# An encoder layer's MLP: the second transposing transfer a step pair later, and another block order in the down projection

## The chip, the cores and the metric

The kernel runs on one NeuronCore of a Trainium2 chip. The metric is the device time of one execution in microseconds (us). Before the change three executions took 1333.12, 1335.69 and 1338.51 us; their median, 1335.69 us, is the time that the change is held against.

## What is computed

One layer of a hybrid encoder: x has 256 tokens of 2048 features, float32. An attention mixer comes first (a combined input projection, two attention branches, gates, an output projection). Its code is not touched. The last part is the MLP, which the change concerns:

```python
h = rms_norm(x, norm_mlp_pre[l])
u = jnp.square(jax.nn.relu(jnp.einsum('bsd,df->bsf', h, w_up[l])))
x = x + rms_norm(jnp.einsum('bsf,fd->bsd', u, w_down[l]), norm_mlp_post[l])
```

w_up is 2048 x 8192 and w_down 8192 x 2048, both float32. We call the two products Up and Down.

## The kernel before the change

**Products in three parts.** Every float32 operand is split into a high part (rounded to the tensor engine's fp32r type, on ScalarE: ACT) and a low remainder (on VectorE: DVE). A product of two 128-row blocks is three matmuls: high by high, high by low, low by high (`Products.add`, L786, matmuls at L793). All of Up and Down runs in *steps*. A step has one weight tile of 128 x 4 x 512 elements (1 MB), that is a 2 x 2 pattern of blocks against a 2 x 2 pattern of activation blocks. A step is done either in eight block products (`eight`, 24 matmuls) or, after Strassen, in seven (`seven`, 21 matmuls) with sums of blocks on both sides. Each weight tile is loaded on SyncE's queue (SP, L700) and split on ACT and DVE (L710 and L712, or L715 to L729 for a step in seven), two steps before its use (`Weights.next`).

**Up** goes through eight groups of 1024 columns, each in eight steps, order `UPS`: weight tiles 1, 2, 0, 4, 3, 6, 5, 7, of which 0 and 3 are steps in seven. The text names steps by n = 0 to 7. A group has two *column groups* (cg) of 512 columns; there are NG = 16 of them. The result z of a group (after ReLU) is turned into operands for Down while the next group runs (`up_each`): `sent` copies the two 16-bit halves of z into planes on ACT (L736) and issues a transposing DMA on SP's queue (L738); `joined` puts the halves together again on ACT (L743); a Square follows (L1307); `u_sets` (via `act_sets`, L1168) makes the operand set. Both column groups are sent in step n = 1 and joined in n = 3 and n = 5. The last group's column groups (14 and 15) are turned by matmuls instead (`u_T`), inside Down.

**Operand sets.** An even cg is used in seven: its set is two pairs of tiles (high `ah`, low `al`), one of single blocks and one of sums of blocks (`sm`, on DVE). An odd cg has one pair. A set of an even cg in `FIRST` (12 and 14 before) has one more block, copied and subtracted at L1191 and L1192, because some of its steps are done in eight. Every set is stored to DRAM on GpSimd's queue (`keeph`, `keepl`, L1195), and read again on ACT's queue when it is needed (`act_again`, tiles `bh`, `bl`, L1208).

**Down** makes its 2048 output columns in two halves, g = 0 and 1. Each half sums over the 16 column groups in eight *blocks* of two, four steps a block (`down_steps`), three matmuls a product, in strict order on the tensor engine (`pr.in_order`). The lists `blocks` give the order:

```python
blocks = [[12, 0, 2, 4, 6, 8, 10, 14],      # first half
          [14, 0, 2, 4, 6, 8, 10, 12]]      # second half
```

Block 12 comes first in the first half, with sets that `u_sets` left in memory. While it runs, 14 and 15 are transposed; while the second block runs, `u_sets` makes and stores their sets (14 in its step n = 1, 15 in n = 3). At step n = 0 of every block but the last, `act_again` asks for the next block's sets. The second half begins with the block that ended the first, whose sets are still there.

**What orders the work.** All these tiles (sets, planes, transposed data, weight sums and lows) are *pages* of 4 KB a partition from one pool of 27. The tile framework orders each engine's instructions from the program's order and its own model of time; an instruction that finds no free page waits, and later ones may pass it. So the code's place of a step is where it may begin, not where it runs. On each engine and queue the resulting order is then fixed.

The functions, with the line numbers that the profile uses:

Of the kernel before, what the change touches and what calls it, by code (L numbers as in the profile page):

```python
# [51 lines left out]
def encoder_layer(ctx: ExitStack, tc: tile.TileContext, a, out):  # L52
# [13 lines left out]
    def page(shape, dt, name):  # L66
        return pages.tile(shape, dt, tag="pg", name=name)
# [673 lines left out]
    def joined(got, dst):  # L741

        nc.scalar.copy(  # L743
            dst.rearrange("p k q -> p (k q)")
            .bitcast(U16)
            .rearrange("p (k t q h) -> p t h k q", k=4, t=2, h=2),
            got.rearrange("p (t h k) q -> p t h k q", t=2, h=2),
        )
# [411 lines left out]


    NG = DFF // 512
    FIRST = (NG - 4, NG - 2)

    def seven_of(cg):
        return cg % 2 == 0

    def act_sets(cg, u):  # L1168


        srcs = []
        if seven_of(cg):
            a11, a21 = u[:, 0:2, :P], u[:, 0:2, P:]
            a12, a22 = u[:, 2:4, :P], u[:, 2:4, P:]
            sums = page([P, 4, 2, P], F32, f"sm{cg}")
            nc.vector.tensor_sub(sums[:, 0], a21, a22)
            nc.vector.tensor_sub(sums[:, 1], a11, a21)
            nc.vector.tensor_sub(sums[:, 2], sums[:, 0], a11)
            nc.vector.tensor_add(sums[:, 3], a12, sums[:, 2])
            own = [(slice(0, 1), a11.unsqueeze(1)),  # L1180
                   (slice(1, 3), u[:, 2:4].rearrange("p k (t q) -> p t k q", t=2))]
            if cg in FIRST:
                own.append((slice(3, 4), a21.unsqueeze(1)))
            srcs = [([P, 1 + len(own), 2, P], own), ([P, 4, 2, P], [(slice(0, 4), sums)])]
        else:
            srcs = [([P, 4, T], [(slice(0, 4), u)])]
        got = []
        for i, (shape, pieces) in enumerate(srcs):
            hi, lo = page(shape, F32R, f"ah{cg}{i}"), page(shape, F32R, f"al{cg}{i}")
            for at, src in pieces:  # L1190
                nc.scalar.copy(hi[:, at], src)  # L1191
                nc.vector.tensor_sub(lo[:, at], src, hi[:, at].bitcast(F32))  # L1192
            for n, part in (("h", hi), ("l", lo)):
                kd = dram.tile(shape, F32, name=f"keep{n}{cg}{i}", tag=f"keep{n}{cg}{i}")
                nc.gpsimd.dma_start(kd, part.bitcast(F32))  # L1195
                kept[cg, i, n] = (shape, kd)
            got.append([hi, lo])
        return got

    def act_again(cg, g):  # L1200

        out = []
        for i in range(2 if seven_of(cg) else 1):
            got = []
            for n in "hl":
                shape, kd = kept[cg, i, n]
                t = page(shape, F32R, f"b{n}{g}{cg}{i}")
                nc.scalar.dma_start(t.bitcast(F32), kd)  # L1208
                got.append(t)
            out.append(got)  # L1210
        return out

    sets = {}
# [27 lines left out]
    def u_sets(cg, u):  # L1241

        got = act_sets(cg, u)
        if NG - 4 <= cg < NG - 2:
            sets[0, cg] = got

    def u_piece(t, half, ps, summed, z):
# [18 lines left out]
            )  # L1266
    wd = a["w_down"].rearrange("(g h j p) c -> p h g j c", h=2, j=2, p=P)

    blocks = [[NG - 4] + list(range(0, NG - 4, 2)) + [NG - 2], [NG - 2] + list(range(0, NG - 2, 2))]

    def down_steps(g, bi):
        b = blocks[g][bi]
# [11 lines left out]
    for g in range(DFF // 1024):  # L1284
        z = Late(lambda g=g: [page([P, 2, 512], F32, f"u{g}{t}") for t in range(2)])

        def up_each(n, g=g, uz=uz):
            if not g:
                first_up(n)
                if n == 7:  # L1290
                    for i in (0, 3, 5):
                        f = page([P, 2, T], F32, f"h2f{i}")
                        for k in range(2):
                            d = hT2[i][:, k].bitcast(F32)
                            nc.vector.tensor_add(f[:, k], d[:, :T], d[:, T:])
                        h2sum[i] = sums_of(f[:, 0], f[:, 1], f"h2s{i}")
                return
            by_dma = g < DFF // 1024 - 1
            for c in range(2):
                cg = g * 2 - 2 + c  # L1300
                if by_dma and c in (0, 1):
                    if n == (1, 1)[c]:
                        uh[cg] = sent([uz[t][:, c] for t in range(2)], f"u{cg}")
                    if n == (3,5)[c]:
                        us[cg] = page([P, 4, T], F32, f"u{cg}")
                        joined(uh[cg], us[cg])
                        nc.scalar.activation(us[cg], us[cg], AF.Square)  # L1307
                elif n == c + 1:
                    us[cg] = u_T(cg, uz)
            steps = (3, 5) if by_dma else (1, 2)  # L1310
            if n in steps:
                cg = g * 2 - 2 + steps.index(n)
                u_sets(cg, us[cg])

        wide_group(
            f"u{g}",
            ups(g),
            uw,
            h2stat7,
            h2stat8,  # L1320
            (1, 2, 3, 7),
            z,
            partial(u_piece, z=z),
            each=up_each,
            turn=None if g else turn_rows,
            after={} if g else {2: scaled[0]},
        )
        uz = z
# [133 lines left out]
    for g in range(2):  # L1462
        pr = Products(f"p{g}", (1, 2, 3, 7))
        pr.in_order = True
        for bi, b in enumerate(blocks[g]):
            end = bi == len(blocks[g]) - 1
            for n, (cg, j, seven) in enumerate(down_steps(g, bi)):
                w = uw.next()
                if g == 0 and bi == 0 and n in (1, 2):
                    us[NG - 3 + n] = u_T(NG - 3 + n, uz)  # L1470
                if g == 0 and bi == 1 and n % 2:
                    u_sets(NG - 2 + n // 2, us[NG - 2 + n // 2])
                if n == 0:
                    for c in range(2):
                        if not end:
                            sets[g, blocks[g][bi + 1] + c] = act_again(blocks[g][bi + 1] + c, g)
                        elif not g:
                            sets[1, b + c] = sets[0, b + c]
                if g == 1 and bi == 5 and n == 0:
                    gp2 = [page([P, 1024], F32, f"gp2{h}") for h in range(2)]  # L1480
                    for h in range(2):
                        nc.sync.dma_start(
                            gp2[h],
                            a["g_mlp_post"][:, h * 1024 : (h + 1) * 1024].partition_broadcast(P),
                        )
                if end and g and n == 0:
                    x3 = [page([P, 1024], F32, f"x3{i}") for i in range(4)]
                    for i in range(4):
                        nc.scalar.dma_start(x3[i], kept["x", i])
                if g == 1 and bi == 6:  # L1490
                    gain(0, n // 2, n % 2)
                    if n % 2:
                        first_means(n // 2)
                if seven:
                    final = end and not any(s for _, _, s in down_steps(g, bi)[n + 1 :])
                    pr.seven(partial(dstat7, sets[g, cg], j), w, final)
                    if final:
                        for t in range(2):
                            zw[g, t] = page([P, 2, 512], F32, f"zw{g}{t}")
                        pr.combine([zw[g, t] for t in range(2)])  # L1500
                    continue
                last = end and n == 3
                if g and end and n > 1:

                    ahead = [*ahead, (cg, j, w)] if last else [(cg, j, w)]
                    if not last:
                        continue
                else:
                    ahead = [(cg, j, w)]
                for which in range(4):  # L1510
                    for m, (cc, jj, ww) in enumerate(ahead):
                        pr.eight(
                            partial(dstat8, sets[g, cc], cc, jj), ww, which, last and m == len(ahead) - 1
                        )
                    if last:
                        bank_, t, half = PLAIN[which]
                        if g:
                            last_piece(t, half, pr.ps[bank_])
                        else:
                            down_piece(g, t, half, pr.ps[bank_])  # L1520
# [61 lines left out]
```

## Time and profile before

| | |
|---|---|
| median of three executions | 1335.69 us |
| the profiled execution's own time | 1333.76 us |
| its span in the trace, first to last instruction | 1332.0 us (the other 1.8 us lie around it) |
| DVE busy, ACT busy | 1075.1 us (81%), 816.1 us (61%) |
| DMA traffic over the span | 346.33 MB, 260 GB/s on average |
| Up from group 2 on, Down's first half, its second half | 730 to 988, 988 to 1158, 1158 to 1323 us from the span's start |

In the profile PE is the tensor engine's matmuls, PEld its weight loads, and `SPq` or `ACTq` a DMA issue on that engine's queue. A row `1055.07:1058.48` of the windows view gives the stretch in us from the span's start. Matmul durations overlap (a matmul of 512 columns is listed with 0.39 us), so what counts on PE is the distance from start to start. The row of a matmul ends with the idle time ahead of it and, behind an arrow, what released it. `PEclk` is the granted share of the tensor engine's clock. In a Down weight's name such as `d040` the digits are the half (0), the column group (4) and the step's index j (0); `d0141` is half 0, column group 14, j = 1.

### The profile page before, as it was taken

The numbers are of one execution on the slowest core, as the hardware profiler recorded it, in microseconds if no ns is written. First come the engines' busy times: TensorE is split into PE (matmuls) and PEld (weight loads), VectorE is DVE, ScalarE is ACT, GpSimd is POOL, SyncE is SP. The second block draws the span as 40 slices with busy tenths as digits, with TensorE's granted clock in tenths as the row PEclk, the third lists the DMA queues.
The fourth block names the chain that finished last, engine by engine and source line by source line (L and its number), as shares of the span: only waits on it lengthen the run. The fifth ranks groups of instructions, "written<-read, shape, count | busy, mean of one in ns | idle before, by whom it ended". The sixth has DMA issues, their size and how long they took to land.

```text
span 1332.0 us, 16065 instructions
## 1 busy us (share of the span) xinstructions
PE 1319.7 (99%) x6163; PEld 1100.9 (83%) x6163; DVE 1075.1 (81%) x1245; ACT 816.1 (61%) x909; POOL 39.2 (3%) x73
## 2 busy tenths in 40 slices
PE   9999999999999999999999999999999999999997
PEld 8888888888888888888888888888888788888886
DVE  7968866777778879885678788888878888898886
ACT  6657584754554665554477788788755555555542
POOL 0000000000000000000100000000100000000000
PEclk9999999999999999999999999999999999999999
DMA  9885766665565667567658888888897998698895
GB/s 347 276 227 173 226 190 187 208 184 169 178 221 190 208 203 252 190 212 265 219 195 274 288 281 286 310 291 278 290 357 289 391 358 332 236 383 330 349 360 201
DMA packets 155917, 346.33 MB, mean 260 GB/s; under 512 B 58560, under 2 KB 59072, under 8 KB 155840
## 3 DMA queue, kind: packets, MB, share of 16 engines
q1 hardware_dynamic: 136160, 276.36, 61.6%
q10 hardware_dynamic: 12960, 43.26, 8.5%
q0 software_dynamic: 6720, 25.69, 4.7%
q8 instruction: 48, 0.79, 0.2%
q14 instruction: 29, 0.24, 0.0%
HBM read 307.01 MB, written 29.61 MB: 253 GB/s over the span
## 4 chain that ended last, share of the span: by engine, by line
PE 68%; issue 23%; DVE 4%; ACT 3%; DMA 2%; POOL 0%; SPq 0%; POOLq 0%; ACTq 0%; DVEq 0%
PE u L793 19%; PE ga L793 6%; PE gb L793 6%; PE ba L793 3%; PE bb L793 3%; PE y L793 3%; PE qn_p L224 2%; PE ka_p L224 2%; PE kn_p L224 2%; PE qa_p L224 2%; PE p L793 1%; PE qn_p L226 1%; PE ka_p L226 1%; PE vn_p L267 1%; PE vn_p L268 1%
## 5 line engine op out<-in xcount | busy, mean ns | idle before, releaser
L224 PE MATMUL qn_p<-hT,qn_h 128*128 128x512 f32 x128 | 45.5, 398 | 0.0
L793 PE MATMUL u<-u_1h,h2T 128*128 128x512 f32 x128 | 43.8, 393 | 1.5 <-DVE u L1250 1.3
L224 PE MATMUL ka_p<-hT,ka_h 128*128 128x512 f32 x128 | 45.0, 396 | 0.0
L224 PE MATMUL kn_p<-hT,kn_h 128*128 128x512 f32 x128 | 44.9, 397 | 0.0
L224 PE MATMUL qa_p<-hT,qa_h 128*128 128x512 f32 x128 | 44.2, 405 | 0.1
L793 PE MATMUL u<-u_2h,h2T 128*128 128x512 f32 x128 | 43.2, 391 | 0.0
L793 PE MATMUL u<-u_5h,h2T 128*128 128x512 f32 x128 | 41.9, 389 | 0.0
L793 PE MATMUL u<-u_6h,h2T 128*128 128x512 f32 x128 | 41.8, 389 | 0.0
L793 PE MATMUL u<-u_4h,h2T 128*128 128x512 f32 x128 | 41.5, 391 | 0.0
L793 PE MATMUL u<-u_7h,h2T 128*128 128x512 f32 x128 | 40.7, 389 | 0.0
L226 PE MATMUL qn_p<-hT,qn_l 128*128 128x256 f32 x128 | 35.9, 281 | 0.0
L226 PE MATMUL kn_p<-hT,kn_l 128*128 128x256 f32 x128 | 35.5, 280 | 0.0
L226 PE MATMUL ka_p<-hT,ka_l 128*128 128x256 f32 x128 | 34.9, 281 | 0.0
L226 PE MATMUL qa_p<-hT,qa_l 128*128 128x256 f32 x128 | 32.5, 282 | 0.1
L793 PEld LDWEIGHTS u<-u_1h,h2T 128*128 128x128 f32 x128 | 24.0, 188 | 8.3 <-ACT u L1307 3.4
L743 ACT COPY u<-u_g 128x2048 uint16<-128x2048 uint16 x12 | 30.3, 2527 | 0.0
L224 PEld LDWEIGHTS qn_p<-hT,qn_h 128*128 128x128 f32 x128 | 24.1, 188 | 5.6
L146 DVE TENSOR_TENSOR y_l<-y_w,y_h 128x1024 fp32r<-128x1024 f32 x16 | 19.0, 1222 | 11.9 <-ACT y_h L138 11.9
L712 DVE TENSOR_TENSOR u_4l<-u_4r,u_4h 128x2048 fp32r<-128x2048 f32 x8 | 18.3, 2293 | 12.5 <-ACT u_4h L710 12.5
L712 DVE TENSOR_TENSOR u_7l<-u_7r,u_7h 128x2048 fp32r<-128x2048 f32 x8 | 18.3, 2293 | 12.5 <-ACT u_7h L710 12.5
L224 PEld LDWEIGHTS kn_p<-hT,kn_h 128*128 128x128 f32 x128 | 23.8, 188 | 5.5
L224 PEld LDWEIGHTS qa_p<-hT,qa_h 128*128 128x128 f32 x128 | 24.0, 192 | 5.1 <-ACT qa_h L144 0.3
(1624 smaller groups left out, 4568.3 us busy)
## 6 DMA issues: line engine op xcount, KB each, us to landing
bh<-keeph ACTq DMA_DIRECT2D x30, 512.0 KB, 9.2
bl<-keepl ACTq DMA_DIRECT2D x30, 512.0 KB, 11.1
keeph<-ah POOLq DMA_DIRECT2D x18, 512.0 KB, 4.8
keepl<-al POOLq DMA_DIRECT2D x18, 512.0 KB, 4.7
va_w<-in_w_in SPq DMA_DIRECT2D x8, 1024.0 KB, 5.5
qn_w<-in_w_in SPq DMA_DIRECT2D x8, 1024.0 KB, 5.2
kn_w<-in_w_in SPq DMA_DIRECT2D x8, 1024.0 KB, 5.1
vn_w<-in_w_in SPq DMA_DIRECT2D x8, 1024.0 KB, 5.1
```

The costliest lines, as they stand in the source:

```text
L146: sub = nc.vector.tensor_sub(lo[part], src, hi[part].bitcast(F32)).ins
L224: nc.tensor.matmul(ps[b], hi[:, k % 4, cs], mv, start=(k == 0), stop=False)
L226: nc.tensor.matmul(ps[b][:, :T], lo[:, k % 4, cs], mv[:, :T], start=False, stop=(k == nk - 1))
L267: nc.tensor.matmul(ps[t], sh, hi[:, k % 4], start=(k == 0), stop=False)
L268: nc.tensor.matmul(ps[t], sh, lo[:, k % 4], start=False, stop=False)
L712: nc.vector.tensor_sub(l1, raw, h1.bitcast(F32))
L743: nc.scalar.copy(dst.rearrange("p k q -> p (k q)") .bitcast(U16) .rearrange("p (k t q h) -> p t h k q", k=4, t=2, h=2), got.rearrange("p ( ...
L793: ins = nc.tensor.matmul(self.ps[i], st, mv[:, blk], start=i not in self.begun, stop=last and n == 2).ins
```

## The change

Four edits. The second column group of an Up group is sent in step n = 2 and not in n = 1. Block 14 moves from the end of the first half to the third place; its sets (now kept by `u_sets`, since its condition takes all cg from 12 on) are used where they were made and aren't read again in the first half. Block 10 now ends the first half and begins the second; 14 comes seventh in the second half and is read again there. `FIRST` is 12 and 10 accordingly, so the additional block belongs to cg 10 and not to cg 14.

```diff
-    FIRST = (NG - 4, NG - 2)
+    FIRST = (NG - 4, NG - 6)
...
         got = act_sets(cg, u)
-        if NG - 4 <= cg < NG - 2:
+        if NG - 4 <= cg:
             sets[0, cg] = got
...
-    blocks = [[NG - 4] + list(range(0, NG - 4, 2)) + [NG - 2], [NG - 2] + list(range(0, NG - 2, 2))]
+    blocks = [
+        [NG - 4, 0, NG - 2] + list(range(2, NG - 4, 2)),
+        [NG - 6] + list(range(0, NG - 6, 2)) + [NG - 2, NG - 4],
+    ]
...
-                    if n == (1, 1)[c]:
+                    if n == (1,2)[c]:
                         uh[cg] = sent([uz[t][:, c] for t in range(2)], f"u{cg}")
...
                         if not end:
-                            sets[g, blocks[g][bi + 1] + c] = act_again(blocks[g][bi + 1] + c, g)
+                            ahead_of = blocks[g][bi + 1]
+                            if g or ahead_of != NG - 2:
+                                sets[g, ahead_of + c] = act_again(ahead_of + c, g)
                         elif not g:
                             sets[1, b + c] = sets[0, b + c]
```

So the orders are now, first half: 12, 0, 14, 2, 4, 6, 8, 10; second half: 10, 0, 2, 4, 6, 8, 14, 12. The weights are asked for in the same orders.

## The prediction

> **What bounds the kernel now.** I read the page first, then the waits of PE, then windows cut at the first matmul of a group or block, and at last the timelines around the gaps.
>
> ```profile
> PE 1319.7 (99%) x6163; PEld 1100.9 (83%) x6163; DVE 1075.1 (81%) x1245; ACT 816.1 (61%) x909; POOL 39.2 (3%) x73
> ```
>
> PE works nearly all the time, and the change neither adds nor drops a matmul, so it can only move idle time and stretches in which PE runs below its pace. The waits of PE give the idle time (us in total, times, longest):
>
> ```profile
> PE x_last L1415 <- ACT by_rows L1412: 2.2, 1, 2.2
> PE p L793 <- DMA bl<-keepl: 1.5, 1, 1.5
> PE u L793 <- DVE u L1250: 1.3, 4, 0.5
> ...
> PE u L793 <- ACT u L1307: 0.2, 1, 0.2
> ```
>
> The first is the kernel's tail, which the change leaves alone. The second is one wait in Down (`p`) for sets that are read back. The third and fourth are five short waits in Up (`u`) at the seams between groups. The windows give what these cost altogether; their columns are the stretch, its length, the engines' busy times, then PEclk, DMA share and GB/s:
>
> ```profile
> 730.07:943.56 213.49, 212.03 (x932) 174.09 (x930) 180.61 (x170) 173.18 (x146) 16.14 (x30) 1.00 0.87 291
> 1031.80:1052.46 20.66, 20.56 (x91) 16.73 (x90) 18.54 (x16) 12.42 (x10) 1.06 (x2) 1.00 1.01 380
> 1052.46:1076.38 23.92, 22.38 (x90) 18.07 (x91) 20.91 (x18) 10.74 (x8) 0.00 (x0) 0.93 1.02 407
> 1055.07:1058.48 3.41, 3.41 (x10) 2.67 (x9) 3.38 (x5) 1.53 (x3) 0.00 (x0) 0.50 1.04 422
> 1117.18:1137.58 20.40, 20.40 (x91) 16.89 (x90) 17.09 (x15) 10.48 (x8) 0.00 (x0) 1.00 0.89 350
> ```
>
> The last row is a Down block (10) at full pace: 20.40 us for 21 + 24 + 21 + 24 = 90 matmuls, 0.2267 us each. Against it, block 2 (second row) takes 0.26 us more and block 4 (third row) 3.52 us more: **3.78 us** lost around one wait. The first row is Up's groups 2 to 6. A group has 6 x 24 + 2 x 21 = 186 matmuls, 42.16 us at that pace; five make 210.80, and the row has 213.49: **2.69 us** lost at five seams. These 6.5 us are all that the edits can reach; 0.5% of the time is 6.7 us, and that is about what a measurement of this kernel can tell from no change.
>
> **The lost time in Down.** PE where block 4 begins:
>
> ```profile
> 1052.77 0.39 PE L793 MATMUL p<-d040l,bh 128*128 128x512 f32 x1
> 1054.70 0.50 PE L793 MATMUL p<-d040h,bl 128*128 128x512 f32 x1 [1.54 <-DMA bl<-keepl]
> ...
> 1055.85 0.63 PE L793 MATMUL p<-d040h,bl 128*128 128x512 f32 x1
> 1056.28 0.63 PE L793 MATMUL p<-d040h,bh 128*128 128x512 f32 x1
> ```
>
> The third matmul of the block waits for the low part of its set. Behind the wait the matmuls start 0.43 us apart in place of 0.23 (last two rows): that is the stretch 1055.07:1058.48, in which the granted clock was 0.50 for 3.41 us, worth up to 1.7 us. The wait of 1.5 us thus cost more than twice its length. [...]
>
> Why were the data late? ACT's queue issued block 4's reads at the time of the first row, a regular block's at that of the second; the other two rows are their median times to landing in us, in that order:
>
> ```profile
> 1042.27 0.33 ACTq L1208 DMA_DIRECT2D bh<-keeph  x1
> 1121.34 0.38 ACTq L1208 DMA_DIRECT2D bh<-keeph  x1
> bl<-keepl ACTq DMA_DIRECT2D x2, 512.0 KB, 12.9
> bl<-keepl ACTq DMA_DIRECT2D x3, 512.0 KB, 12.0
> ```
>
> Block 4's reads go out 10.5 us after block 2 began (1031.80), the regular ones 4.2 us after their block began (1117.18). 4.2 + 12.0 us fit into 20.4 with some 4 us to spare, 10.5 + 12.9 don't. The delay I read as one of pages. While block 0 runs, the pool has to hold 6 pages of its sets, 6 of block 2's, which is already being read, some 9 for the making of 14 and 15 (six of sets, one of sums, two of u) and up to 8 for two steps' weights in seven: 29 of 27. So 15's set is late, it keeps its pages into block 2's time, and block 4's reads wait. The transfers are crowded as well (window 1010:1035):
>
> ```profile
> DMA packets 2373, 8.64 MB, mean 346 GB/s; under 512 B 203, under 2 KB 203, under 8 KB 2372
> ...
> d021r<-in_w_down SPq DMA_DIRECT2D x1, 1024.0 KB, 14.6
> ```
>
> **Down's edits.** With 14 third, nothing is read during block 0. Its pages then are 29 - 6 = 23, and of the 8.64 MB some 2.8 (2 reads of 384 and 4 of 512 KB) go. During block 14 the pool holds its 6 pages, 6 for block 2's reads and 8 for weights. Block 2's reads, now the first after the opening, then find pages at once, as in a regular block. So I count the whole **-3.78 us**; the bound on the other side is 0, if the wait comes back in front of block 2. I take the first, because the regular row with its 4 us of reserve is the nearer one.
>
> In place of a read, PE now waits for the making of the sets. These rows are of that making and of PE's second step of the third block:
>
> ```profile
> 1032.98 1.49 ACT L715 CAST d021h<-d021r 128x1536 fp32r<-128x1536 f32 x1
> 1034.37 1.04 ACT L1191 CAST ah<-u 128x1024 fp32r<-128x1024 f32 x1
> 1036.18 1.22 DVE L1192 TENSOR_TENSOR al<-u,ah 128x1024 fp32r<-128x1024 f32 x1
> 1036.56 0.39 PE L793 MATMUL p<-d030h,bh 128*128 128x512 f32 x1
> ```
>
> Set 15 ends at 1036.18 + 1.22 = 1037.40, and the step that will use it begins at 1036.56. At today's times PE would stand 0.8 us, and with it all that is queued behind it, since its order in Down is strict; with a clock stretch of 1.7 us that is 2.5. But ACT makes set 15 behind the split of `d021r`, and that load took 14.6 us beside the reads that now go. If it takes 8 or 9, some 6 us are gained against 0.8 needed. I count 0, bounds 0 and +2.5.
>
> The second half keeps its pattern: sets in memory first, six blocks that are read, and a block with the additional part last. Block 14 is read where 10 was, with the same sizes; block 10 ends the first half with the sizes that 14 had. I count 0, under the cover of the same 4 us.
>
> `FIRST` gives cg 10 one more block of 128 x 256 in group 6, a copy on ACT and a subtraction on DVE of this length:
>
> ```profile
> 960.12 0.42 DVE L1192 TENSOR_TENSOR al<-u,ah 128x256 fp32r<-128x256 f32 x1
> ```
>
> DVE is late at the seams, so I count it on the path: **+0.42 us**, once. What cg 14 saves lies off the path: 0.
>
> **Up's edit.** Group 5, as an example of 2 to 6:
>
> ```profile
> 874.32 1.99 ACT L736 COPY u_s<-u 128x1024 uint16<-128x1024 uint16 x2
> 876.34 2.01 SPq L738 DMA_TRANSPOSE u_g<-u_s  x1
> 876.66 1.22 DVE L716 TENSOR_TENSOR u_3t<-u_3r 128x1024 f32<-128x1024 f32 x1
> 877.91 1.05 ACT L728 CAST u_3eh<-u_3t 128x1024 fp32r<-128x1024 f32 x1 [1.60 <-DVE u_3t L716]
> 878.45 0.54 SPq L700 DMA_DIRECT2D u_7r<-in_w_up  x1
> 879.61 1.91 ACT L710 CAST u_5h<-u_5r 128x2048 fp32r<-128x2048 f32 x1 [0.64 <-PE u L793]
> 884.77 1.89 ACT L710 CAST u_7h<-u_7r 128x2048 fp32r<-128x2048 f32 x1
> 900.87 0.47 PE L793 MATMUL u<-u_1h,h2T 128*128 128x512 f32 x1 [0.26 <-DVE u L1250]
> ```
>
> The second column group's copies (first row) stand in the code ahead of weight 3's sums `u_3t`. These need nothing but the loaded weight and two pages, and yet they start behind the copies, and ACT waits 1.60 us for them. I read that as pages again: the transfer (planes and landing page) takes them first. A pair later, `u_3t` takes them first. ACT's 1.60 us then hold its first `u_3eh`, and the copies (1.99 us) fit into 1.60 + 0.64 us of idle time ahead of `u_5h`, which PE releases and which can't come sooner. From there one chain over ACT and DVE leads to the seam. It gets shorter by at most one `u_3eh` (1.05 us), if that too slips ahead of `u_5h`, and 2.69 / 5 = 0.54 us a seam would do. On SP the transposing issue holds the queue 2.01 us, and `u_7r` goes out behind it; it may now go ahead. Weight 1 and 2 of the next group come later on that queue and have time. Bounds: all seams closed, -2.69; or the copies land behind `u_5h` and push the chain by 1.99 - 0.64 = 1.35 us at five seams, +6.75. I take half of the gain, **-1.35**, because the idle time of the row 877.91 is where the copies would go.
>
> **Sum.** -3.78 + 0.42 - 1.35 = -4.71 us. The profiled execution's own time is 1333.76, so it would be 1329.05. The median of the runs is 1.93 us above the profiled execution; with the same distance the forecast is 1335.69 - 4.71 = **1331.0 us**.
>
> **The rivals.**
> 1. *Up's edit changes nothing in time.* For it: both transfers stand in step 1, but the second already runs behind the split of weight 6, that is, no sooner than a pair later. Then 1335.69 - 3.78 + 0.42 = 1332.3.
> 2. *Down's wait comes back at block 2.* For it: the stores of 14 and 15 still go out there, and its sets' pages stay until block 14 ends. Against it: six fewer pages asked for. 1335.69 + 0.42 - 1.35 = 1334.8.
> 3. *Slower: the copies fall behind `u_5h`.* The place is ACT in each of groups 2 to 6; it decides from the point at which the copies start later than 879.61 - 1.99 = 877.6 in group 5's terms, 3.3 us later than today. Price +6.75: 1335.69 - 3.78 + 0.42 + 6.75 = 1339.1. Against it: 2.24 us of idle time ahead of that point.
> 4. *More goes than the profiled execution shows.* Its median stands 1.93 us higher; if that is late reads too, they go with the crowding, and all seams close: 1335.69 - 3.78 + 0.42 - 2.69 - 1.93 = 1327.7.
> 5. *The half clock isn't the wait's doing* and stays, so that Down gives 3.78 - 1.7 = 2.08: 1335.69 - 2.08 + 0.42 - 1.35 = 1332.7. Against it: it follows right on the only wait of Down. [...]
>
> **How the numbers follow.** The forecast gets 0.45; the rivals, in order, 0.17, 0.10, 0.11, 0.12 and 0.05. The range takes in the forecast, rivals 1, 2 and 5 with the runs' own scatter (some 2.5 us to either side of the median), and rival 4's 1327.7: 1327.5 to 1337.0. Rival 3 is left out. Faster by over 0.5% (under 1329.0) is rival 4 and the lower edge of the forecast, 0.12 + 0.08 = 0.20. Slower by over 0.5% (above 1342.4) needs rival 3 and more: 0.05. The rest, 0.75, is within 0.5%.
>
> **What would show it.** Right: no wait of PE for `bl` in Down, all its blocks at 20.40 us, no stretch at 0.50 before the tail; set 15 ready before the third block's second step; in Up, `u_3t` starting before the second copies, and five groups in less than 213.49 us. Wrong: PE waiting for `al` in Down, the same wait ahead of block 2, `u_5h` starting behind the copies, or seams longer than 0.54 us.

## The result, and the profile after the change

Six executions of the changed kernel took 1325.66 to 1326.09 us, median **1325.88 us**. Six of the kernel before took 1333.12 to 1338.51, median 1333.77. The ratio of the two means is 0.9934, 95% interval 0.992 to 0.9949: faster by 0.66%. That set of before was a high one: all its six executions lie at 1333.12 us or above, and of the 60 that ran beside the experiments 16 do. Against the median of those 60, 1331.97 us, the change is worth 6.1 us, 0.46%. The prediction said 1331.0, with a range from 1327.5; the result lies 1.6 us under that range. The profiled execution took 1325.66 us (span 1323.9).

The engines' line of the page after the change, and the three largest waits of PE (us in total, times, longest):

```profile
PE 1314.7 (99%) x6163; PEld 1099.1 (83%) x6163; DVE 1073.9 (81%) x1245; ACT 815.6 (62%) x909; POOL 39.2 (3%) x73
```

```profile
PE x_last L1418 <- ACT by_rows L1415: 2.2, 1, 2.2
PE idle L174 <- POOL ones L164: 1.0, 1, 1.0
PE qa_p L224 <- DVE hT L308: 0.5, 1, 0.5
```

No wait for `u` or `p` is left. The windows after the change, cut at the same matmuls as before: groups 2 to 6; group 7 and block 12; Down from block 0's first matmul to that of the last block's second step; and block 2 by itself:

```profile
729.48:940.28 210.80, 210.80 (x932) 174.55 (x930) 179.46 (x170) 171.07 (x145) 15.03 (x28) 1.00 0.88 289
940.28:1007.87 67.59, 67.59 (x315) 56.20 (x314) 54.77 (x52) 42.03 (x42) 4.25 (x8) 1.00 0.84 300
1007.87:1298.91 291.04, 291.04 (x1285) 240.99 (x1284) 250.28 (x214) 153.65 (x124) 3.23 (x6) 1.00 0.88 339
1048.67:1069.07 20.40, 20.40 (x91) 16.89 (x90) 16.98 (x14) 9.64 (x7) 0.00 (x0) 1.00 0.95 361
```

The two rows of the kernel before that the prediction doesn't show:

```profile
943.56:1011.40 67.84, 67.84 (x315) 56.19 (x315) 56.42 (x54) 41.70 (x42) 4.25 (x8) 1.00 0.81 295
1011.40:1306.22 294.82, 293.18 (x1285) 242.01 (x1284) 249.96 (x214) 154.05 (x125) 3.19 (x6) 0.99 0.89 345
```

In every row of after PE is busy for the whole stretch: no idle time is left in them to gain. The 8.10 us between the two profiled executions (1333.76 - 1325.66) split into 2.69 in groups 2 to 6, 0.25 in group 7 and block 12, 3.78 in Down, 0.59 ahead of group 2 (730.07 against 729.48) and 0.79 behind the last cut (25.78 against 24.99 us to the end of the span). The last two I take for scatter of single executions. The first is there already at group 1's start (687.46 against 686.86 us), ahead of which the code is the same, and in the runs below group 2 begins between 729.36 and 730.45 us. The second arises behind PE's last matmul, which starts 20.30 us behind the cut in both; in the runs below this end takes 25.0 to 25.4 us where the last block has no wait.

So the profile moved where the prediction looked, and by its sizes in Down. But which edit did it?

### The profile page after: what moved, and what is told of

Its sections match the earlier page's. It is cut to its first block, busy times and chain, and to the rows that moved or that the text cites. A ratio compares the mean times of both kernels' runs of the same rounds, so it can differ in the third digit from the quotient of the medians.

```text
span 1323.9 us, 16049 instructions
## 1 busy us (share of the span) xinstructions
PE 1314.7 (99%) x6163; PEld 1099.1 (83%) x6163; DVE 1073.9 (81%) x1245; ACT 815.6 (62%) x909; POOL 39.2 (3%) x73
## 4 chain that ended last, share of the span: by engine, by line
PE 52%; issue 43%; POOL 2%; DMA 1%; DVE 1%; ACT 1%; SPq 0%; POOLq 0%; ACTq 0%; DVEq 0%
PE ga L793 6%; PE gb L793 6%; PE u L793 5%; PE ba L793 3%; PE bb L793 3%; PE y L793 3%; PE qn_p L224 2%; PE ka_p L224 2%; PE qa_p L224 2%; PE kn_p L224 2%; PE qn_p L226 1%; PE ka_p L226 1%; PE vn_p L267 1%; PE vn_p L268 1%; PE y_p L267 1%
## 5 line engine op out<-in xcount | busy, mean ns | idle before, releaser
L793 PEld LDWEIGHTS u<-u_6h,h2T 128*128 128x128 f32 x128 | 24.0, 188 | 5.0
L793 PEld LDWEIGHTS u<-u_7h,h2T 128*128 128x128 f32 x128 | 24.0, 188 | 5.0
```

The source lines that it names most:

```text
L793: ins = nc.tensor.matmul(self.ps[i], st, mv[:, blk], start=i not in self.begun, stop=last and n == 2).ins
```

## The experiments

The table at the end has two of these stretches, groups 2 to 6 and Down, for each kernel, and the waits of PE in them. "Theory O" in the texts means that the orders which the framework fixed on each engine decide. The kernel before ran beside each set: its medians were 1331.99 (15 executions), 1331.95 (17), 1332.29 (15) and 1331.7 us (13). Where one execution is told, its profile is the evidence.

### Each half alone

**e_up**: the kernel before with only `n == (1, 1)[c]` changed to `n == (1,2)[c]`.

> The kernel before with the Up edit alone (second column group's transfer a pair later; Down and FIRST as before). Theory A, the two edits are worth what their own windows show and add up: Up gives back its seams, 2.69 us (groups 2 to 6 in 210.8 us, no wait of PE for u in them), and Down keeps its 3.78 us with the wait for bl: 1333.77 - 2.7 = 1331.1 us, and in the trace the copies stand behind u_5h and the first sum of a group starts some 38.3 us after the group, not 41.8. Theory B, the seams were closed by what the Down edit takes out of Up (cg 14's additional block, fewer pages): the five groups take 213.5 us and the time is 1333.8. Theory C, half of the profile's distance to the other runs was late reads that the Up edit moves too: under 1330.0.

Measured: 1326.3 us (1326.22 to 1327.1), ratio 0.9955 (0.9943 to 0.9968). That is the time of the whole change. Windows of this kernel, groups 2 to 6 and Down:

```profile
729.81:940.61 210.80, 210.80 (x932) 174.55 (x930) 179.15 (x169) 170.85 (x144) 15.12 (x28) 1.00 0.88 288
...
1008.20:1299.24 291.04, 291.04 (x1285) 241.07 (x1284) 249.66 (x214) 154.05 (x125) 3.20 (x6) 1.00 0.90 350
```

Down takes 291.04 us with the *old* block order. None of the three theories had that: the Up edit also removed the wait in Down.

**e_down**: the kernel after with that edit undone, so Down's edits and `FIRST` alone.

> The kernel after with the Up edit undone (Down's edits and FIRST alone). Theory A: Down gives 3.78 us (all of its blocks 20.40 us, no wait for bl, no stretch at half clock behind the start), Up keeps its 2.69 us: 1333.77 - 3.78 = 1330.0 us, and 1330.4 with the prediction's 0.42 us for cg 10's additional block if that is on the path (the seam behind group 6, or what the seven windows of Up sum to, is then 0.42 us longer than before). Theory B, Down needs Up's edit to come off (set 15 is late otherwise, or block 2's reads): a wait of PE for al or bl of 1 to 2.5 us is there, and the time is 1331 to 1333.

Measured: 1335.3 us (1334.28 to 1338.23), ratio 1.0026 (1.0016 to 1.0035), *slower* than before. Its windows and its waits of PE:

```profile
729.41:943.96 214.55, 212.07 (x932) 174.11 (x930) 180.92 (x171) 171.12 (x146) 16.15 (x30) 1.00 0.87 287
943.96:1013.84 69.88, 68.90 (x315) 55.90 (x315) 53.20 (x50) 42.21 (x42) 4.26 (x8) 1.00 0.80 296
1013.84:1308.00 294.16, 291.65 (x1286) 240.91 (x1284) 251.89 (x217) 154.77 (x125) 3.24 (x6) 1.00 0.87 336
```

```profile
PE p L793 <- DVE al L1192: 1.6, 1, 1.6
PE u L793 <- ACT u_0h L715: 1.5, 1, 1.5
...
PE p L793 <- DVE d0130l L712: 1.0, 1, 1.0
PE p L793 <- DVE d0140el L729: 0.9, 1, 0.9
```

The wait for `bl` is gone, as forecast, and others stand in its place: for set 15 (`al`), at the seam of groups 6 and 7 (`u_0h`), and for two weights' lows. So the two edits don't add up: -5.7 and +3.3 us alone, and together no more than the first by itself (1325.88 and 1326.3 us, with the same two windows).

### What closes the seams in Up

In the kernel after, group 5 starts at 855.96. ACT around the second column group's copies (`u_s`):

```profile
877.28 1.91 ACT L710 CAST u_5h<-u_5r 128x2048 fp32r<-128x2048 f32 x1 [0.74 <-PE u L793]
879.10 1.99 ACT L736 COPY u_s<-u 128x1024 uint16<-128x1024 uint16 x2
880.99 1.90 ACT L710 CAST u_7h<-u_7r 128x2048 fp32r<-128x2048 f32 x1
882.80 2.51 ACT L743 COPY u<-u_g 128x2048 uint16<-128x2048 uint16 x1
...
887.44 1.92 ACT L710 CAST u_1h<-u_1r 128x2048 fp32r<-128x2048 f32 x1
889.25 1.04 ACT L1191 CAST ah<-sm 128x1024 fp32r<-128x1024 f32 x1
```

The copies *do* fall behind `u_5h`. But the other orders moved as well: the join (`u<-u_g`, 2.51 us) stood ahead of `u_7h` before and now stands behind it, and `u_1h` stands ahead of the cast of the sums. Two runs undo one of these each, with a line that makes a weight's split on ACT wait for a given instruction:

```diff
-                    self.got.append(pair_weights(*args, **kw, after=after.get(n)))
+                    first = behind_of.get(args[1])
+                    with tc.issue_after(first) if first else nullcontext():
+                        self.got.append(pair_weights(*args, **kw, after=after.get(n)))
```

**e_u1sums** adds to it `behind_of[f"u{cg // 2 + 2}_1"] = cast`, where `cast` is the cast of the sums in `act_sets` (`ah<-sm`).

> The kernel after, in Up with the next group's u_1h on ACT held behind the second cast of the sums (as before), all else free; DVE's order ahead of the seam is then that of the kernel before (u_1l, a sum's part, u_2l, the rest, the first sum), while the join stays behind u_7h. Theory A, a sum of delays: u_2l goes ahead of the sums, 1.2 us, so that the first one starts some 39.5 to 40 us after the group instead of 38.3, still ahead of 41.3: groups 2 to 6 in 210.8 us. Rival B, the join's place decides: 210.8 too. Rival C, DVE's order alone makes the seam: 0.5 us at each of the five, 213.5 us.

Measured: 1329.55 us, groups 2 to 6 in 213.01 us. DVE ahead of the seam, first in the kernel after, then in this one (its group 5 starts at 857.07):

```profile
892.73 0.68 DVE L821 TENSOR_TENSOR u<-u,u 128x512 f32<-128x512 f32 x1
893.45 0.69 DVE L822 TENSOR_TENSOR u<-u,u 128x512 f32<-128x512 f32 x1
894.24 0.69 DVE L1250 TENSOR_TENSOR u<-u,u 128x512 f32<-128x512 f32 x1
...
896.04 2.28 DVE L712 TENSOR_TENSOR u_2l<-u_2r,u_2h 128x2048 fp32r<-128x2048 f32 x1
```

```profile
895.20 0.68 DVE L825 TENSOR_TENSOR u<-u,u 128x512 f32<-128x512 f32 x1
896.06 2.29 DVE L712 TENSOR_TENSOR u_2l<-u_2r,u_2h 128x2048 fp32r<-128x2048 f32 x1 [0.18 <-ACT u_2h L710]
898.27 0.68 DVE L826 TENSOR_TENSOR u<-u,u 128x512 f32<-128x512 f32 x1
898.87 0.68 DVE L1256 TENSOR_TENSOR u<-u,u 128x512 f32<-128x512 f32 x1
```

`u_1l`, later now, pushes the first part (L825) back, and DVE puts the 2.29 us of `u_2l` in front of the rest. The sum that PE waits for (L1250, here L1256) starts 38.28 us after its group in the kernel after, and 41.80 here, as before (41.83). Theory A's 39.5 to 40 was wrong: one swap of two casts brings back 2.21 of the 2.69 us. That is rival C's time, but not its cause alone: PE's order at these seams (weights 1, 2, 0 behind weight 7) is again that of before, too.

**e_u7join** adds `behind_of[f"u{g}_7"] = join` for the first column group's join.

> The kernel after, in Up with weight 7's split on ACT held behind the first column group's join (as before), all else free; ACT then makes u_5h, the rest of weight 3, the copies, the join, u_7h. Theory A, a sum of what ACT and DVE have to do ahead of the seam: u_7h comes some 3.7 us later than in the kernel after, the casts behind it some 1.2 us, and DVE puts u_2l (1.2 us) ahead of the group's sums, so that the first sum starts some 40.7 us after the group instead of 38.3; before it was 41.8 with 0.54 us lost, so that this is just not late: groups 2 to 6 in 210.8 to 211.3 us. Rival B, the join ahead of u_7h alone was the seam's cause: 0.54 us or more at each seam, groups 2 to 6 in 213.5 us or more. Rival C, only DVE's order counts (u_2l ahead of the sums): likewise 213.5 here, and in the next kernel too.

Measured: 1334.2 us, groups 2 to 6 in 218.06 us: worse than before. PE at the seam behind group 5:

```profile
901.90 0.39 PE L797 MATMUL u<-u_7h,h2T 128*128 128x512 f32 x1
903.86 0.50 PE L797 MATMUL u<-u_0h,h2T 128*128 128x512 f32 x1 [1.56 <-ACT u_0h L715]
```

Behind weight 7 PE's own fixed order now has weight 0 first, whose split on ACT starts only when PE has done weight 7 (the cast is 1.48 us long in before's group 5, and PE stood for 1.56). In the kernel after the order there is 1, 2, 1, 2, 0. Theory A fell here too; the loss fits rival B in sign, but by the row it comes about by PE's order.

**e_u3** and **e_u22** are the kernel after with `n == (1,3)[c]` and `n == (2,2)[c]`.

> The kernel after with the second column group's transfer a pair later still (n = 3). Theory O, the seam's loss follows from the fixed orders, PE's included: where PE takes up weight 0 first behind weight 7 it waits some 1.7 us (the split of weight 0 needs the buffer that weight 7 leaves), where it takes 1, 2, 0 it loses 0.35 to 0.65 us as before, where 1, 2, 1, 2, 0 nothing. In this kernel's order the seams ahead of groups 3 to 7 are: none, 0.35 to 0.65, 1.7, 1.7, 0.35 to 0.65: 4.1 to 4.7 us more than after, some 1330.3 us, if Down keeps its 20.40 us blocks. Theory L, later is better for the same reason as in the edit (the copies leave weight 3's sums and ACT free): no seam has a loss, 1326.

> The kernel after with both column groups' transfers in step n = 2. PE's fixed order at the seams ahead of groups 3 to 7: weights 1, 2, 1, 2, 0 (no loss expected), 1, 2, 0 twice (0.34 to 1.7 us, as such seams had so far), 0 first (1.7 us), 1, 2, 1, 2, 0 (none). Theory O (the fixed orders decide): 2.4 to 5.1 us more than after, 1328.3 to 1331. Theory L (later transfers free ACT for weight 3's sums): 1326.

Measured: 1338.21 us, groups 2 to 6 in 217.54 us; and 1341.41 us, 226.15 us. Where PE has weight 0 first, e_u3 lost the 1.7 us expected, but its two other seams lost 1.2 and 1.7 instead of 0.35 to 0.65, and e_u22 lost 15.4 us over the five groups instead of 2.4 to 5.1 (in it the clock was granted at 0.50 for 3.41 us from 862.31, and at 0.98 over the five groups, worth some 4.5 us of their 226.15). Theory O has the direction, but neither the size of a seam nor each of them (e_u22 lost 1.6 us at weight 2's low, at a seam forecast without loss); theory L (later is better) is out.

### What made the wait in Down

**e_set15** is the kernel before with the lines above in `Weights.next` and `behind_of["d021"] = cast` for set 15's cast.

> The kernel before with one order changed on ACT in Down: the split of d021 waits for the making of set 15's high part (ah), so that ah goes ahead of it, as in the kernel with the Up edit alone; DVE follows. Up, the block order, the reads, the pages asked for and the loads are as before. Theory O (an order on ACT: set 15 stood behind the split of a weight whose load took 14.6 us, kept its pages, and block 4's reads waited for them): set 15 is made some 4 to 8 us earlier than 23.0 us after block 0's start, block 4's reads go out 6 to 8 us after block 2's start in place of 10.5, PE doesn't wait for bl, the stretch at half clock is gone, all blocks take 20.40 us: the time is some 3.8 us less than the profiled execution of before, 1330.0, with Up's seams as they were. Theory P (the prediction: pages of the reads that lie in block 0's time, and their traffic): both are as before, so that the wait of about 1.5 us at block 4 and the 3.8 us stay: 1332 to 1334.

Measured: 1331.28 us (1329.25 to 1335.34), ratio 0.9995 (0.9984 to 1.0007). Block 4's reads went out 8.7 us after block 2's start (before 10.5), and the wait stayed, in two parts:

```profile
PE p L797 <- DMA bl<-keepl: 1.7, 1, 1.7
...
PE p L797 <- DMA bh<-keeph: 0.8, 1, 0.8
```

So set 15's place alone isn't the cause. The first of block 2's reads left 2.3 us after block 0's start, as before.

**e_d001** changes one place in the kernel before (d001's high part, and on DVE the subtraction that needs it, come behind the casts of its sums), and the framework then draws Down's other orders on ACT as in e_up by itself. **e_order** forces them: e_d001's lines, e_set15's, and `behind_of["d011"] = read` for block 2's last read in `act_again`. Up is untouched in both.

```diff
+        first_h = name != "d001"
+        if first_h:
             nc.scalar.copy(h1[:, 1:4], raw[:, 1:4])
...
-            nc.scalar.copy(h2[i], t[i])
+            last_e = nc.scalar.copy(h2[i], t[i]).ins
             nc.vector.tensor_sub(l2[i], t[i], h2[i].bitcast(F32))
+        if not first_h:
+            with tc.issue_after(last_e):
+                nc.scalar.copy(h1[:, 1:4], raw[:, 1:4])
```

> The kernel before with Down's orders on ACT and DVE made those of the kernel with the Up edit alone (d001's sums are cast ahead of its high part, d011's split comes behind block 2's reads, d021's behind set 15's high part); PE, SP and all of Up are as before, and so are the block order, the pages asked for and the bytes. Theory O (Down's fixed orders made the wait; the Up edit only changed them): block 2's reads go out some 0.3 us after block 0's start in place of 2.3, block 4's some 7 us after block 2's start in place of 10.5, PE doesn't wait for bl, no stretch at half clock, all blocks 20.40 us: some 3.8 us less than the profiled execution of before, 1328 to 1330. Theory L (the lateness of ACT and DVE that Up's seams leave behind makes it, whatever Down's orders): the wait of 1 to 2 us at block 4 stays, 1331 to 1334.

> The kernel before with a single thing changed: for d001 (third step of block 0), the casts of its sums stand ahead of the cast of its high part on ACT; the framework then draws the other orders of the run with three forced orders by itself. Theory O1 (this one place starts the chain: d001's high part waits for the buffer that block 12's last step leaves, and held up the sums and block 2's reads behind it): block 2's reads go out some 0.3 us after block 12's end in place of 2.3, no wait for bl, Down from block 0 to the last block 291.04 us as in the kernel after (before 294.82), about 1329.2 us. If it takes more than that place, a wait of over 0.5 us stays.

Measured: 1329.21 us (1328.6 to 1329.46), ratio 0.9975 (0.9966 to 0.9984); and 1329.31 us (1329.08 to 1329.68), ratio 0.9977 (0.9966 to 0.9987). In both, Down takes 291.04 us, and groups 2 to 6 as long as before (213.32 and 213.48). In medians they are 3.1 and 2.4 us under the kernel before beside them: the 3.78 us belong to its profiled execution, and its others scatter. ACT at block 12's end, first in the kernel before (block 0 starts at 1011.40), then in e_d001 (1011.42):

```profile
1011.64 1.49 ACT L715 CAST d001h<-d001r 128x1536 fp32r<-128x1536 f32 x1 [2.57 <-issue]
1013.02 1.05 ACT L728 CAST d001eh<-d001t 128x1024 fp32r<-128x1024 f32 x1
1013.71 0.33 ACTq L1208 DMA_DIRECT2D bh<-keeph  x1
1013.98 1.91 ACT L710 CAST d011h<-d011r 128x2048 fp32r<-128x2048 f32 x1
```

```profile
1011.10 1.05 ACT L731 CAST d001eh<-d001t 128x1024 fp32r<-128x1024 f32 x1 [2.01 <-DVE d001t L720]
1011.69 0.33 ACTq L1219 DMA_DIRECT2D bh<-keeph  x1
...
1012.06 1.48 ACT L735 CAST d001h<-d001r 128x1536 fp32r<-128x1536 f32 x1
...
1015.02 1.92 ACT L710 CAST d011h<-d011r 128x2048 fp32r<-128x2048 f32 x1 [1.48 <-issue]
```

The first of block 2's reads (`bh`) leaves 2.3 us after block 12's end before, and 0.3 us after it in e_d001. What those 2 us mean is seen in the DMA share of block 0's first half, before and in e_d001:

```profile
1011.40:1021.60 10.20, 10.20 (x47) 8.45 (x45) 8.49 (x11) 6.17 (x7) 1.06 (x2) 1.00 0.89 295
```

```profile
1011.42:1021.62 10.20, 10.20 (x47) 8.45 (x45) 9.84 (x13) 6.12 (x7) 1.60 (x3) 1.00 0.98 361
```

Behind this stretch there is little room to make up the 0.7 MB that weren't moved here (66 GB/s x 10.2 us): up to block 4 the DMA share is 0.97 to 1.03 in every 5.1 us before, and 1.01 to 1.03 in e_up, whose first read left 0.3 us after block 12's end too. So lateness stays: the last of block 2's reads lands 22.1 us after block 0's start before, and 17.3 us after it in e_d001; block 4's reads go out 10.5 and 6.3 us after block 2's start (1031.82 in e_d001, first read at 1038.08). The links between are read from the two traces; no run tests each of them.

**e_d011** has only `behind_of["d011"] = read`, which puts d011's split behind block 2's reads; d001 stays as it was.

> The kernel before with d011's split on ACT held behind block 2's reads; d001's high part stays ahead of its sums, and set 15's cast stays behind d021's split. Theory O1 (d001's place): the reads still wait for d001's two casts, go out over 1.5 us after block 12's end, and PE waits at block 4 for 0.5 to 2 us (1330 to 1334). If the place of d011 is what counts: no wait, Down 291.04 us, 1329.2.

Measured: 1330.52 us, Down 292.28. The first read left 0.30 us after block 12's end, and PE didn't wait for `bl`. ACT at block 12's end (block 0 starts at 1011.02):

```profile
1011.27 1.48 ACT L717 CAST d001h<-d001r 128x1536 fp32r<-128x1536 f32 x1 [2.57 <-issue]
1011.32 0.33 ACTq L1219 DMA_DIRECT2D bh<-keeph  x1
...
1012.65 1.05 ACT L731 CAST d001eh<-d001t 128x1024 fp32r<-128x1024 f32 x1
```

So my expectation was wrong in naming d001's place: d011's does it too, because the framework then put the first reads ahead of `d001eh`. What e_d001 and e_d011 share is that one cast of d001 stands ahead of the first read at block 12's end (`d001eh` in the one, `d001h` in the other), where before both do. In e_d011 set 15 still stands behind the split of d021, so that its place isn't needed for the wait to go. The trace of e_d011 has one wait behind the 1.24 us that it still loses, 0.9 us for the low of d020.

### Pages and traffic, the prediction's reasons

**e_hold** is the kernel after with six pages held from block 0 to block 14 (filled with one column); **e_fill** fills them with whole reads of block 2's sets; **e_crowd3** puts back the bytes alone, as copies of those sets from DRAM to DRAM (`nc.scalar.dma_start(kx, kd)`, held behind d010's split). (A first run of that last kernel, e_crowd2, had matmuls at about a third of their pace, those of `qn_p` listed with 1.09 us where before has 0.40, 3987.78 us in all, and tells nothing.)

```diff
+                if g == 0 and bi == 1 and n == 0:
+                    held = [page([P, 4, T], F32, f"held{i}") for i in range(6)]
+                    for h in held:
+                        nc.scalar.dma_start(h[:, 0, 0:1], kept["x", 0][:, 0:1])
```

> The kernel after with six pages held from block 0 to block 14 of the first half (six fills of one column, read again by ACT), as many as the reads took there before. Theory P (pages): sets 14 and 15 are late, or block 2's reads find no page before the six are given back: they go out over 8 us after block 14's start, and PE waits 1 to 4 us ahead of block 2 (1327 to 1330). Theory O: set 15 stays ahead of d021's kind of split on ACT, and block 2's reads come in time or less than 1 us late: 1326 to 1327.

> The kernel after with both things put back that the block order took from block 0's time: six pages held to block 14, as in the run that held pages alone, and filled with whole reads of block 2's kept sets (2.8 MB on ACT's queue; nothing uses them). Orders as in the run with pages alone, in which the fourth read of block 2's sets landed 1.3 us before its use. Theory P (traffic, the prediction's other half): 2.8 MB at about 420 GB/s are 6.8 us of all DMA engines; what the idle shares of blocks 0 and 14 don't take up arrives late: a wait of 1 to 4 us ahead of block 2 or for al in block 14, 1328 to 1331. Theory O (orders alone): no wait, 1326 to 1327.

> The kernel after with the traffic alone put back: six copies from DRAM to DRAM of the size of the reads that left block 0's time (2.8 MB) go out on ACT's queue there; nothing reads them, and no pages are asked for. Theory P (traffic): a wait of 1 to 2 us in block 14 or ahead of block 2, Down over 292 us. Theory O (orders, with the run that put back pages and bytes as its witness): Down from block 0 to the last block 291.0 to 291.5 us, 1326 to 1327.5 in all.

Measured: 1326.95, 1327.23 and 1327.14 us. Their rows of Down, in this order:

```profile
1008.58:1299.62 291.04, 291.04 (x1285) 241.07 (x1284) 249.88 (x214) 154.97 (x130) 3.23 (x6) 1.00 0.88 340
```

```profile
1008.35:1299.81 291.46, 291.38 (x1286) 240.85 (x1284) 249.63 (x214) 154.83 (x130) 3.21 (x6) 1.00 0.90 348
```

```profile
1008.06:1299.98 291.92, 291.38 (x1285) 240.91 (x1284) 249.46 (x214) 154.10 (x124) 3.24 (x6) 1.00 0.89 344
```

Pages cost nothing, pages and bytes 0.42 us, and bytes alone, which went out some 5.5 us earlier, 0.88 us. With these orders, what Down's edit takes out of block 0's time is worth under 0.9 of the 3.78 us.

### What Down's edits cost by themselves

**e_down15** is e_down with `behind_of["d0141"] = cast` for set 15's cast. **e_first** is the kernel before with `FIRST = (NG - 4, NG - 2, NG - 6)`: cg 10's additional block is made, and not used.

> The kernel after with the Up edit undone (which had waited 1.6 us for al of set 15 in block 14, and lost 1.8 there) and one order on ACT changed: d0141's split waits for the making of set 15's high part, as in the kernel after. Theory O: set 15 is ready some 4 us earlier, the wait for al goes, the other two waits at Down's start (0.9 and 1.0 us, for lows of d0140 and d0130) stay: 1.8 us less than the profiled run of that kernel, some 1333.2. Theory L (lateness carried from Up): set 15's source itself is late, and the wait stays above 1 us: 1335.

> The kernel before, with the additional block of cg 10 made as well (FIRST has 12, 14 and 10; the block isn't used, and is stored and read with its set). This prices the block alone. If it is what cost 1.26 us more at the seam between groups 6 and 7 in the run without the Up edit: 1.6 to 1.7 us lost there in place of 0.42. The prediction's price was 0.42 us more, 0.84. If the loss there came from the other block order: 0.42 as before. Down's orders move too, so its wait may be another one.

Measured: 1333.41 us (1333.2 expected): the wait for `al` is gone, and Down takes 293.04 us instead of 294.16. And 1337.1 us. PE at the seam behind group 6, before and in e_first:

```profile
942.90 0.39 PE L793 MATMUL u<-u_7h,h2T 128*128 128x512 f32 x1
943.56 0.47 PE L793 MATMUL u<-u_1h,h2T 128*128 128x512 f32 x1 [0.27 <-DVE u L1250]
```

```profile
943.08 0.39 PE L793 MATMUL u<-u_7h,h2T 128*128 128x512 f32 x1
944.99 0.47 PE L793 MATMUL u<-u_1h,h2T 128*128 128x512 f32 x1 [1.52 <-ACT u_0h L715]
```

From start to start 1.91 against 0.66 us: the block costs 1.25 us there, by the orders that it moves, three times the 0.42 us of its instruction. Most of the rest of e_first's loss lies in Down's first and last block, with waits of 0.95 and 1.2 us for the lows of d0130 and d1131.

### All kernels

| kernel | time, us | groups 2 to 6 | Down from block 0 | waits of PE in these two |
|---|---|---|---|---|
| before, profiled | 1333.76 | 213.49 | 294.82 | `u`, `bl` |
| after | 1325.88 | 210.80 | 291.04 | none |
| e_up | 1326.3 | 210.80 | 291.04 | none |
| e_down | 1335.3 | 214.55 | 294.16 | `u`, `u_0h`, `al`, lows |
| e_u1sums | 1329.55 | 213.01 | 292.27 | `u`, a low of d0141 |
| e_u7join | 1334.2 | 218.06 | 291.04 | `u_0h` |
| e_u3 | 1338.21 | 217.54 | 294.24 | `u`, `u_0h`, `al`, lows |
| e_u22 | 1341.41 | 226.15 | 291.04 | `u`, a low of u_2 |
| e_set15 | 1331.28 | 213.24 | 295.70 | `u`, `bl`, `bh` |
| e_order, e_d001 | 1329.21, 1329.31 | 213.32, 213.48 | 291.04, 291.04 | `u` |
| e_d011 | 1330.52 | 213.56 | 292.28 | `u`, a low of d020 |
| e_hold | 1326.95 | 210.80 | 291.04 | none |
| e_fill | 1327.23 | 210.79 | 291.46 | none over 0.2 |
| e_crowd3 | 1327.14 | 210.80 | 291.92 | `bl` |
| e_down15 | 1333.41 | 214.60 | 293.04 | `u`, `u_0h`, lows, `bl` |
| e_first | 1337.1 | 214.54 | 294.07 | `u`, `u_0h`, lows, `bl` |

## Why the prediction was wrong

Three steps failed: the cause given to Down's term, the limit set to Up's term, and the distance from the profiled execution to the median.

**What bounds the kernel** was right for the profiled execution: the 2.69 and the 3.78 us lost were nearly all there was to gain in it, and all of it came, with 0.25 us more in group 7 and block 12.

**Down's term**, -3.78, has the right size and the wrong cause. "The delay I read as one of pages" and "the transfers are crowded as well" were put back and cost 0 to 0.88 us, and e_order and e_d001, which have the pages and the bytes of before, lose nothing in Down; so the block order, to which the term was given, isn't needed. Rival 2 is out with it. The late reads began a block earlier than the prediction looked: at block 2's reads, whose first left 2.3 us after block 0's start, behind two casts of d001 on ACT, where 0.3 us is possible (e_d001, e_d011); and not at set 15 (e_set15). The DMA rows of the stretch ahead of the gap would have pointed there. That the term's size came out is luck: the other half of the change brought it.

**"I count 0, bounds 0 and +2.5" for set 15**, and **+0.42 for cg 10's block**: neither is paid in the kernel after. In e_down both are: PE waits 1.6 us for `al`, and the block costs 1.25 us at a seam without reserve. Both were taken as prices of their instructions; they depend on the orders around them.

**Up's term**, -1.35, failed at "one chain over ACT and DVE leads to the seam. It gets shorter by at most one `u_3eh`". What the term began with came true: `u_3t` starts ahead of the copies, 13.2 us after group 5's start instead of 18.5 (that pages had held it back wasn't tested). Rival 3's condition was met all the same, the copies fell behind `u_5h`, and the first column group's Square ends 30.44 us after the group's start instead of 29.41. But rival 3's price of +6.75 had the wrong sign: the group's first sum came 3.55 us earlier, by the orders behind the Square. The prediction held the rest of the order fixed, and the framework drew all of it anew, on PE too. Worth 1.34 us of the error. Rival 1 is out.

**The half clock** went with the wait: without the wait it is gone (1.00 granted over Down in e_order, e_d001 and e_up, 0.99 before). Rival 5 is out.

**The 1.93 us** between the profiled execution and the median was carried over, and had no ground. Kernels that wait in Down scatter (before 1329.94 to 1338.51, e_set15 1329.25 to 1335.34, e_down 1334.28 to 1338.23); those that don't keep within 0.9 us (after 0.43, e_d001 0.60). The median of the first three executions was high: the 60 beside the experiments have medians of 1331.7 to 1332.29, set by set. Why that first set lay higher stays open. Rival 4 came nearest with its 1327.7 us. Its reason, late reads that vary, fits the spreads of the kernels that wait for `bl`, though no run shows it directly, and e_down scatters without a wait for a read in its trace.

The account: 1331.0 - 1325.88 = 5.12 us. Up 1.34, group 7 and block 12 0.25, cg 10's block 0.42, the start 0.59, the end 0.79, and, the largest, the distance to the median 1.71 (1.93 forecast, 1325.88 - 1325.66 = 0.22 found): 5.10 together, the rest is rounding.

What stays open: why the framework draws an order that closes the seams with the transfer in step 2 and bad ones in step 3 or with both in step 2. The runs show the orders and what they cost, not how they come about.

## What to carry to other kernels

Where a framework orders the engines, an edit is first of all a new order, everywhere behind it: compare the two orders, instruction by instruction and on PE too, before pricing the lines that were edited. When a read is late on full DMA engines (a share of 0.97 to 1.03 here), go back to where they last had room (0.89 here), and look at what stood ahead of the issue there. And run each half of a change alone: here one half did all the work, and the other by itself made the kernel slower.

## What the runs showed of the hardware

The DMA issues in ACT's queue went out in that queue's order with the casts: with one cast more ahead of it, the first read of block 2 left 2.0 us later (1013.71 against 1011.69 us, with block 0 starting 0.02 us apart).

In these runs a wait's length did not by itself tell whether the clock fell. It was granted at 0.50 for 3.41 us behind 1.54 us of idle time (before); behind 0.80 and 1.69 us (e_set15) the matmuls came to start 0.43 us apart, as there. And it was granted at 1.00 over the stretches, groups 2 to 6 or Down, that have single waits of 1.56 (e_u7join), 1.6 (e_down) and 1.7 us (e_u3). Why it fell behind 1.54 us once and not behind 1.7 us, the runs leave open.
